# A macaron layer on one core: SwiGLU's block sums are issued one matrix later, weight sums wait behind bank copies, weight sums are cast by halves, modulation sums are spread later

## The chip, the cores and the metric

The kernel runs on one core of a Trainium2 chip. The time is the device time of one execution in microseconds (us); the number that counts is the median of the runs, and beside it stands one execution recorded by the hardware profiler. The engines in the text: PE (TensorE, matmuls), PEld (its weight loads), DVE (VectorE), ACT (ScalarE), POOL (GpSimd) and SP (SyncE, which here issues DMAs). Each engine works through its own instructions in order and waits on semaphores; SP's DMA issues wait in SP's order too.

## What is computed

One layer for 1024 positions of width 1024: a SwiGLU half step, a token mixer (two kinds of attention), and a second SwiGLU half step, each with a norm before and after and a modulation by a vector `c`. Cut to what the change touches:

```python
def swiglu(u, w_gate, w_up, w_down):          # u (1024, 1024), D_FF = 2816
    return (jax.nn.silu(u @ w_gate) * (u @ w_up)) @ w_down
...
h = x + 0.5 * g1 * postRMS(SwiGLU_1(mod1(preRMS(x))))    # FFN1
h = h + g2 * postRMS(Mixer(mod2(preRMS(h))))
h = h + 0.5 * g3 * postRMS(SwiGLU_2(mod3(preRMS(h))))    # FFN2
```

The shifts, scales and gates of `mod1` to `mod3` and g1 to g3 are rows of c @ w_ada (1024 by 9216). All arrays are float32.

## The kernel before, in words

Every float32 product runs as three matmuls on halves of the operands: `halves` makes a high part H (a cast on ACT, L217) and a low part L (a subtraction on DVE, L218), and `product` issues H·H, H·L and L·H (L293 to L295), each 128x128 by 128x512, for four blocks of 128: 12 matmuls a product.

**Matrices and pairs.** D_FF is cut into 11 pieces; for each, a pair of a gate and an up matrix is multiplied with u. `Matrix` is one of these. It does not take eight 512-products but seven, from sums of blocks of weights and of u (a scheme of Strassen's kind). `start` does the two products A11·B11 and A12·B21 (24 matmuls); then p6 (weight sum S2 with T2 of u), p5 (S1, T1), p7 (S3, T3), p3 (S4, B22) and p4 (A22, T4), 12 matmuls each: 84 matmuls a matrix, 168 a pair. T1 to T4 stay in SBUF; a matrix's S1 to S4 are made while it runs. `sums` (L315) loads the blocks (r1, r2), DVE makes `s21` = (S2, S1) at L326 and L327 and `s34` = (S3, S4) at L330 and L331, and `halves` casts both parts of `s21` in one instruction of 1024 columns, and takes its low part in another. `sums34` does the same for `s34`, `last` for A22.

**Banks.** The products accumulate in two PSUM banks in turn, `bank` and `bank2`. Each can go on only when its partial result has been read: C11 by an ACT copy (L360) and a DVE add (L368), C12 by an ACT copy (L388) and an add (L403), C22 by an ACT copy (`copy(self.c22, self.b)`, L394, which p3 waits for) and a DVE add (L398, which p4 waits for). `out` (L343) applies SiLU on ACT to a gate's block (L347) or multiplies the up block with it on DVE (L350); C21 comes straight from the bank.

**Order.** FFN1 and FFN2 run the same function. The first three pairs (six matrices, m0 to m5) all do `start` first, and `rest_first` does their other products, each matrix asking for the sums of the next one (`nxt.sums`); `done` (`follow` in `ffn`) is called between them. Pairs 3 to 10 run in a loop: `start`, then `rest`. When a pair is complete, `hidden` (L460) makes the four block sums of its SwiGLU result on DVE (L466 to L469) and stores them and three of the blocks to HBM (L472, L483); `down_sums` (L485) loads two pieces of the down weights (L488, L490), makes their four sums (L493 to L496) and stores them (L483). The down products read all that back later. `steps` is a generator of modulation sums: each step loads a row block of w_ada (`wada`, 512 KB, L86, three buffers) and reduces it with `csil` on DVE (L79, `mod_sum`); after eight steps a column of gates is stored to HBM (`g_dram`, L121). `per_pair(c)` says how many steps follow pair c.

A scheduler turns this program into one order for each engine, by dependencies, priorities and estimated costs: where the program names an operation sets its priority, not its place. `tc.issue_after(x)` keeps an operation from being placed ahead of x.

## Time and profile before

| | us |
|---|---|
| runs | 2236.72, 2235.43, 2240.99; median 2236.72 |
| profiled execution | 2242.12 (span 2240.4) |
| granted PE clock, mean | 0.989 |
| PE busy | 2155.7 (96%) |
| DVE busy | 1552.1 (69%) |
| ACT busy | 1050.0 (47%) |

FFN1 fills the span's first 700 us, the mixer the stretch up to 1570, FFN2 the rest. The gate and up products run from about 50 to 487 us and from 1575 to 2010, the down products behind them. How to read it: PE's busy share is high, so the question for each stage is when PE waited, for whom, and what that engine was doing. A row of waits reads "engine line waited for: us in total, times, longest us"; a time line row gives start and duration in us, the instruction, and in brackets the idle time before it and what ended it. A number from a busy share or from counts of matmuls is softer, since a few per cent of the matmul records are missing.

### The profile page before, as it was taken

The page shows a single profiled execution, that of the slowest core. Times are in us where ns is not written, and L with a number is a line of the kernel's source. Part 1 is how long each engine was busy: PE and PEld are TensorE (multiplying, and loading weights), DVE is VectorE, ACT ScalarE, POOL GpSimd, SP SyncE. Part 2 cuts the span into 40 slices and gives each one's busy share as a digit, 9 for nine tenths or more (in the row PEclk, how much of TensorE's full clock was granted, in tenths as well). Part 3 has the DMA queues.
Part 4 walks back from the last instruction along what each step waited for, and adds up shares of the span by engine and source line. Part 5 has one row for each costly group of instructions (what it writes and reads, how often), then busy time and mean ns, then how long its engine had stood idle before and what let it go on. Part 6 is the DMA issues. An engine that isn't in the chain of part 4 may idle for free.

```text
span 2240.4 us, 28449 instructions
## 1 busy us (share of the span) xinstructions
PE 2155.7 (96%) x10328; PEld 1780.0 (79%) x10328; DVE 1552.1 (69%) x2646; ACT 1050.0 (47%) x1893; POOL 61.5 (3%) x84
## 2 busy tenths in 40 slices
PE   6999999999998999999999999999999999999997
PEld 4777788878887877888888988788877788878886
DVE  7979767567577688576677676665985766655566
ACT  6633324235456556455455454565733333334454
POOL 0000000000000011001011000000000000000000
PEclk9999999999999999999999999999999999999999
DMA  8488635359785111110211123653474544538666
GB/s 327 146 281 280 211 130 185 127 183 328 245 291 201 50 45 46 33 54 26 70 55 64 36 94 100 236 202 128 148 239 166 184 173 144 179 111 277 215 224 213
DMA packets 139792, 361.27 MB, mean 161 GB/s; under 512 B 19458, under 2 KB 23682, under 8 KB 139651
## 3 DMA queue, kind: packets, MB, share of 16 engines
q1 hardware_dynamic: 138018, 353.68, 46.4%
q0 software_dynamic: 1632, 5.77, 0.7%
q8 instruction: 81, 1.33, 0.2%
q14 instruction: 61, 0.49, 0.1%
HBM read 270.77 MB, written 88.62 MB: 160 GB/s over the span
## 4 chain that ended last, share of the span: by engine, by line
PE 68%; DVE 19%; DMA 6%; ACT 4%; issue 3%; SPq 0%; DVEq 0%; ACTq 0%
PE bank L295 8%; PE bank L293 7%; PE bank L294 7%; PE pps L841 4%; PE pps L843 4%; PE pps L845 4%; PE bankA L581 3%; PE bankA L582 3%; PE bankA L580 3%; PE bankB L580 3%; PE bankB L582 3%; PE bankB L581 3%; DVE f L1050 2%; DVE wsL L218 2%; DMA wada<-in_wada 2%
## 5 line engine op out<-in xcount | busy, mean ns | idle before, releaser
L841 PE MATMUL pps<-uH,wsH 128*128 128x512 f32 x512 | 209.0, 408 | 0.0
L843 PE MATMUL pps<-uL,wsH 128*128 128x512 f32 x512 | 203.8, 398 | 0.0
L845 PE MATMUL pps<-uH,wsL 128*128 128x512 f32 x512 | 203.2, 397 | 0.0
L218 DVE TENSOR_TENSOR tbL<-stg,tbH 128x512 fp32r<-128x512 f32 x154 | 105.9, 689 | 97.9 <-ACT tbH L217 97.6
L217 ACT CAST tbH<-stg 128x512 fp32r<-128x512 f32 x154 | 95.6, 621 | 141.9 <-DMA stg<-d_T 98.8
L581 PE MATMUL bankA<-tbL,sbH 128*128 128x512 f32 x352 | 139.8, 397 | 6.3 <-DVE tbL L218 6.3
L580 PE MATMUL bankA<-tbH,sbH 128*128 128x512 f32 x352 | 140.1, 398 | 5.5 <-DVE y L656 5.1
L293 PE MATMUL bank<-uH,wsH 128*128 128x512 f32 x352 | 139.1, 401 | 4.1 <-ACT wsH L217 3.5
L294 PE MATMUL bank<-uL,wsH 128*128 128x512 f32 x352 | 140.2, 398 | 1.6 <-DVE uL L748 1.5
L582 PE MATMUL bankA<-tbH,sbL 128*128 128x512 f32 x352 | 139.6, 396 | 0.7 <-DVE sbL L218 0.7
L295 PE MATMUL bank<-uH,wsL 128*128 128x512 f32 x352 | 139.5, 397 | 0.6 <-DVE wsL L218 0.6
L134 DVE TENSOR_TENSOR wsL<-raw,wsH 128x1024 fp32r<-128x1024 f32 x72 | 88.0, 1222 | 68.1 <-ACT wsH L133 67.6
L217 ACT CAST wsH<-s 128x1024 fp32r<-128x1024 f32 x88 | 92.2, 1049 | 85.8 <-DVE s L327 69.8
L217 ACT CAST sbH<-stg 128x512 fp32r<-128x512 f32 (+1 forms) x176 | 98.3, 565 | 62.7 <-DMA stg<-hd_A 47.4
L218 DVE TENSOR_TENSOR sbL<-stg,sbH 128x512 fp32r<-128x512 f32 (+1 forms) x176 | 108.5, 620 | 27.0 <-ACT sbH L217 26.1
L360 ACT COPY q<-bank 128x512 f32<-128x512 f32 x44 | 25.5, 588 | 193.1 <-PE bank L295 193.1
L845 PEld LDWEIGHTS pps<-uH,wsL 128*128 128x128 f32 x512 | 96.6, 189 | 17.7
L218 DVE TENSOR_TENSOR wsL<-s,wsH 128x1024 fp32r<-128x1024 f32 x88 | 107.0, 1217 | 3.5 <-ACT wsH L217 3.2
L841 PEld LDWEIGHTS pps<-uH,wsH 128*128 128x128 f32 x512 | 97.3, 190 | 14.5
L843 PEld LDWEIGHTS pps<-uL,wsH 128*128 128x128 f32 x512 | 97.0, 189 | 14.3
L217 ACT CAST wsH<-raw 128x1024 fp32r<-128x1024 f32 (+1 forms) x88 | 73.3, 834 | 74.0 <-PE bank L294 49.8
L580 PE MATMUL bankB<-tbH,sbH 128*128 128x512 f32 x264 | 102.7, 389 | 0.0
(246 smaller groups left out, 5905.7 us busy)
## 6 DMA issues: line engine op xcount, KB each, us to landing
wada<-in_wada SPq DMA_DIRECT2D x56, 512.0 KB, 5.7
raw<-in_wg SPq DMA_DIRECT2D x50, 512.0 KB, 6.5
raw<-in_wu SPq DMA_DIRECT2D x50, 512.0 KB, 4.6
raw<-in_wd SPq DMA_DIRECT2D x44, 512.0 KB, 4.3
stg<-hd_A SPq DMA_DIRECT2D x88, 256.0 KB, 4.5
stg<-d_S SPq DMA_DIRECT2D x88, 256.0 KB, 3.5
stg<-d_T SPq DMA_DIRECT2D x88, 256.0 KB, 3.9
d_S<-s SPq DMA_DIRECT2D x40, 512.0 KB, 2.7
```

Source lines behind the costliest of these rows:

```text
L134: eng.tensor_sub(l, raw, h.bitcast(F32))
L217: ACT.copy(h, src)
L218: eng.tensor_sub(l, src, h.bitcast(F32))
L293: PE.matmul(ps, H[:, ks], bH, start=first and k == 0, stop=False, skip_group_check=not first)
L294: PE.matmul(ps, H[:, ks], bL, start=False, stop=False, skip_group_check=not first)
L295: PE.matmul(ps, L[:, ks], bH, start=False, stop=k == 3, skip_group_check=not first)
L580: PE.matmul(ps, sH[:, ts], tH, start=first, stop=False, skip_group_check=not check)
L581: PE.matmul(ps, sH[:, ts], tL, start=False, stop=False, skip_group_check=not check)
L582: PE.matmul(ps, sL[:, ts], tH, start=False, stop=last, skip_group_check=not check)
L841: PE.matmul(ps, aH, bH, start=i == 0, stop=False)
L843: PE.matmul(ps, aH, bL, start=False, stop=False)
L845: PE.matmul(ps, aL, bH, start=False, stop=i == n - 1)
```

## The change

Four edits, in gate and up products of both FFNs except the last, which concerns FFN1.

1. In `sums`, the cast of `s21` becomes two of 512 columns on ACT, S1's half first, and its low part two of 512 on DVE, S2's first: 44 more instructions on each of the two engines. `summed` is the last of the sums.
2. In `rest_first`, p7 is written ahead of `nxt.sums`, and these sums may not stand ahead of the ACT copy (`copied`) and the DVE add (`added`) of this matrix's C22.
3. `hidden` of a pair moves from behind the pair to the middle of the next pair's gate matrix (`between`, behind `m.summed`). For c = 4 the third pair's down sums go with it, as before. For the third pair `follow` no longer calls it, and the last pair's is called at the end of the loop.
4. `per_pair` of FFN1 goes from 2, then eight times 4, to 0 for the first three pairs, 5 for six pairs and 4 for one: 34 steps before and after.

```diff
@@ -325,10 +325,17 @@
             self.s34 = s34 = late.tile([P, 2, HALF], F32, name="s34", tag=tag, bufs=4)
             V.tensor_add(s21[:, 1], r2[:, 0], r2[:, 1])
             V.tensor_sub(s21[:, 0], s21[:, 1], r1[:, 0])
-            H, L = halves(wpool, s21.rearrange("p a b -> p (a b)"), "ws", 4, D)
-            self.w["S2"], self.w["S1"] = (H[:, :HALF], L[:, :HALF]), (H[:, HALF:], L[:, HALF:])
+            H = wpool.tile([P, D], F32R, name="wsH", tag="wsH", bufs=4)
+            L = wpool.tile([P, D], F32R, name="wsL", tag="wsL", bufs=4)
+            for j, n in ((1, "S1"), (0, "S2")):
+                h, l = H[:, j * HALF:(j + 1) * HALF], L[:, j * HALF:(j + 1) * HALF]
+                ACT.copy(h, s21[:, j])
+                self.w[n] = h, l
+            for j, n in ((0, "S2"), (1, "S1")):
+                h, l = self.w[n]
+                V.tensor_sub(l, s21[:, j], h.bitcast(F32))
             V.tensor_sub(s34[:, 0], r1[:, 0], r2[:, 0])
-            V.tensor_sub(s34[:, 1], r1[:, 1], s21[:, 0])
+            self.summed = V.tensor_sub(s34[:, 1], r1[:, 1], s21[:, 0])
 
         def sums34(self):
             H, L = halves(wpool, self.s34.rearrange("p a b -> p (a b)"), "ws", 4, D)
@@ -391,11 +398,11 @@
             self.b = self.psum.tile([P, HALF], F32, name="bank2", tag="pb", bufs=1)
             product(self.b, self.w["S1"], block_of("T1"), True)
             self.c22 = self.q()
-            ACT.copy(self.c22, self.b)
+            self.copied = ACT.copy(self.c22, self.b)
 
         def p7(self):
             product(self.bank, self.w["S3"], block_of("T3"), False)
-            V.tensor_add(self.c22, self.bank, self.c22)
+            self.added = V.tensor_add(self.c22, self.bank, self.c22)
             self.out("C22", self.c22)
 
         def p3(self):
@@ -446,9 +453,10 @@
             m.p6()
             done(i - 1)
             m.p5()
+            m.p7()
             if nxt is not None:
-                nxt.sums(late, True)
-            m.p7()
+                with tc.issue_after(m.copied.ins), tc.issue_after(m.added.ins):
+                    nxt.sums(late, True)
             m.p3()
             if nxt is not None:
                 nxt.sums34()
@@ -532,7 +540,7 @@
                 with tc.tile_pool(name="late", bufs=1, side="right", reuse_waits="tile") as late:
                     steps = steps_fn(late)
                     def follow(n):
-                        if n % 2:
+                        if n % 2 and n // 2 < NFIRST - 1:
                             hidden(late, n // 2, mats[n // 2][1].c, hd)
                         if n > 1:
 
@@ -547,11 +555,17 @@
                             if second:
                                 down_sums(fp, late, A[wd][c], c, hd)
                             m.start()
-                            rest(late, m, None if second or c != NFIRST + 1 else
-                                 lambda: down_sums(fp, late, A[wd][NFIRST - 1], NFIRST - 1, hd))
-                        hidden(late, c, mats[c][1].c, hd)
+
+                            def between(m=m, c=c):
+                                with tc.issue_after(m.summed.ins):
+                                    hidden(late, c - 1, mats[c - 1][1].c, hd)
+                                    if c == NFIRST + 1:
+                                        down_sums(fp, late, A[wd][NFIRST - 1], NFIRST - 1, hd)
+
+                            rest(late, m, None if second else between)
                         for _ in range(per_pair(c)):
                             next(steps, None)
+                    hidden(late, NPAIR - 1, mats[NPAIR - 1][1].c, hd)
                     for _ in steps:
                         pass
 
@@ -787,7 +801,7 @@
     def no_steps(mp):
         yield
 
-    pending = ffn("wg1", "wu1", "wd1", start0, pending0, steps1, lambda c: 2 if c == 1 else 4 if c < 10 else 0, steps1b, 0, lambda t: A["x"][t * P:(t + 1) * P, :], lambda t: h_dram[0][t])
+    pending = ffn("wg1", "wu1", "wd1", start0, pending0, steps1, lambda c: 0 if c < 3 else 5 if c < 9 else 4 if c == 9 else 0, steps1b, 0, lambda t: A["x"][t * P:(t + 1) * P, :], lambda t: h_dram[0][t])
 
     pending = mixer(locals())
```

TensorE has the same 10370 instructions in both, in the same order but for four short places: at 60 to 95 us, where the first matrices' products trade places with the transposes of T3 (these begin seven matmuls later), two places in pairs 3 and 4, where the two matmuls with T1's blocks no longer stand ahead of the matmuls with the low part of S2, and two in FFN2. In mixer and down products nothing moves. DVE's modulation sums up to the end of m5 are 18 before and 16 after.

Three places in the engines' orders. On ACT, around the C22 copy of the third pair's gate matrix (m4): `bank_1217` and `bank_1218` are the bank that p5 filled, `s_1236` and `s_1251` the next matrix's `s21`, `s_1237` and `s_1252` its `s34`. Before:

```order
L217 CAST wsH<-raw_1123 128x512
L388 COPY q<-bank 128x512
L217 CAST wsH<-s_1236 128x1024
L394 COPY q<-bank_1217 128x512
L217 CAST wsH<-s_1237 128x1024
L347 ACTIVATE q<-q 128x512
```

After:

```order
L395 COPY q<-bank 128x512
L401 COPY q<-bank_1218 128x512
L354 ACTIVATE q<-q 128x512
L332 CAST wsH<-s_1251 128x512 x2
L217 CAST wsH<-s_1252 128x1024
L354 ACTIVATE q<-bank 128x512
```

The C22 copy (L394, now L401) stood behind the cast of the next matrix's `s21` and stands ahead of its two halves (L332) now.

On DVE, at the gate matrix of pair 3: `s_1446` and `s_1421` are its `s21`, `s_1386` and `s_1441` the block sums of the third pair's SwiGLU result. Before:

```order
L466 TENSOR_TENSOR s_1386<-q 128x512
L468 TENSOR_TENSOR s_1387<-q 128x512
L467 TENSOR_TENSOR s_1386<-s_1386,q 128x512
L326 TENSOR_TENSOR s_1446<-raw_1444 128x512
L469 TENSOR_TENSOR s_1387<-q,s_1386 128x512
L327 TENSOR_TENSOR s_1446<-s_1446,raw 128x512
L330 TENSOR_TENSOR s_1447<-raw,raw_1444 128x512
L368 TENSOR_TENSOR q<-bank_1429,q 128x512
L218 TENSOR_TENSOR wsL<-s_1446,wsH 128x1024
L331 TENSOR_TENSOR s_1447<-raw,s_1446 128x512
```

After, two rows behind the gate's L327:

```order
L336 TENSOR_TENSOR wsL<-s_1421,wsH 128x512
L357 TENSOR_TENSOR q<-q 128x512
L336 TENSOR_TENSOR wsL<-s_1421,wsH 128x512
L410 TENSOR_TENSOR q<-bank_1327,q 128x512
L338 TENSOR_TENSOR s_1422<-raw,s_1421 128x512
L357 TENSOR_TENSOR q<-q 128x512
L79 ISA wada,modcol_2000<-wada,csil,colsT 128x1024
L79 ISA modcol_2000 128x1
L357 TENSOR_TENSOR q<-bank,q 128x512
L218 TENSOR_TENSOR wsL<-s_1422,wsH 128x1024
L218 TENSOR_TENSOR wsL<-raw_1419,wsH 128x512
L474 TENSOR_TENSOR s_1441<-q 128x512
```

`hidden` (L466 to L469) stood ahead of the sums and their low part; now it (from L474) begins behind the two halves of the low part (L336), two bank adds, one modulation sum and the low parts of S3, S4 and A22.

On SP, in FFN2 at pair 4's up matrix (`raw<-in_wu`): `hd_A_3` and `d_S_3` are stores of pair 3's SwiGLU result and its block sums, `d_T_2` and `d_T_4` of down sums, `raw_16265` and `raw_16327` the second load for the latter. Before:

```order
L472 DMA hd_A_3_35_16110<-q 128x512
L483 DMA d_S_3_16112<-s_16100 128x1024
L472 DMA hd_A_3_34_16108<-q 128x512
L483 DMA d_S_3_16114<-s_16101 128x1024
L488 DMA raw<-in_wd 128x1024
L490 DMA raw_16265<-in_wd 128x1024
L483 DMA d_T_2_16188<-t_16182 128x1024
L483 DMA d_T_2_16190<-t_16183 128x1024
L483 DMA d_T_4_16273<-t_16267 128x1024
L483 DMA d_T_4_16275<-t_16268 128x1024
L311 DMA raw<-in_wu 128x1024
```

After:

```order
L480 DMA hd_A_3_33_16230<-q 128x512
L496 DMA raw<-in_wd 128x1024
L480 DMA hd_A_3_35_16234<-q 128x512
L480 DMA hd_A_3_34_16232<-q 128x512
L498 DMA raw_16327<-in_wd 128x1024
L491 DMA d_S_3_16236<-s_16224 128x1024
L491 DMA d_S_3_16238<-s_16225 128x1024
L491 DMA d_T_2_16250<-t_16244 128x1024
L491 DMA d_T_2_16252<-t_16245 128x1024
L491 DMA d_T_4_16335<-t_16329 128x1024
L491 DMA d_T_4_16337<-t_16330 128x1024
L311 DMA raw<-in_wu 128x1024
```

The load of the second down weights stood behind two stores of block sums and stands ahead of them now; the up matrix's load has kept its place behind the four stores of down sums.

## The prediction

> **What bounds the kernel now.** I read the page first, then the list of what PE waits for, stage by stage, then the time line around the largest waits. From the page, the span, the busy times, four groups of instructions and a transfer:

> ```profile
> span 2240.4 us, 28449 instructions
> PE 2155.7 (96%) x10328; PEld 1780.0 (79%) x10328; DVE 1552.1 (69%) x2646; ACT 1050.0 (47%) x1893; POOL 61.5 (3%) x84
> ...
> L218 DVE TENSOR_TENSOR tbL<-stg,tbH 128x512 fp32r<-128x512 f32 x154 | 105.9, 689 | 97.9 <-ACT tbH L217 97.6
> L217 ACT CAST tbH<-stg 128x512 fp32r<-128x512 f32 x154 | 95.6, 621 | 141.9 <-DMA stg<-d_T 98.8
> ...
> L217 ACT CAST wsH<-s 128x1024 fp32r<-128x1024 f32 x88 | 92.2, 1049 | 85.8 <-DVE s L327 69.8
> ...
> L218 DVE TENSOR_TENSOR wsL<-s,wsH 128x1024 fp32r<-128x1024 f32 x88 | 107.0, 1217 | 3.5 <-ACT wsH L217 3.2
> ...
> wada<-in_wada SPq DMA_DIRECT2D x56, 512.0 KB, 5.7
> ```

> TensorE (PE) is busy 96% of the span and the change takes no matmul away, so it can only win where PE stands still. Two windows of 20 us show the price of standing still (columns: length, then busy time and count of PE, PEld, DVE, ACT, POOL, then the granted clock):

> ```profile
> 140.00:160.00 20.00, 15.99 (x69) 12.59 (x68) 17.10 (x26) 6.81 (x10) 0.00 (x0) 1.00 0.85 275
> 160.00:180.00 20.00, 17.10 (x74) 13.74 (x73) 15.06 (x25) 3.01 (x5) 0.00 (x0) 0.98 0.86 322
> 180.00:200.00 20.00, 20.00 (x85) 16.45 (x84) 18.77 (x26) 9.24 (x13) 0.00 (x0) 0.94 0.80 266
> 340.00:360.00 20.00, 20.00 (x90) 16.57 (x89) 12.95 (x18) 8.23 (x12) 0.00 (x0) 1.00 0.55 187
> 1760.00:1780.00 20.00, 18.70 (x74) 14.99 (x75) 10.70 (x14) 6.37 (x8) 0.00 (x0) 0.91 0.42 140
> ```

> A window without a wait holds 90 matmuls, 20/90 = 0.222 us each; twelve of them (a product) take 2.7 us. The others lose by idling and, in three of them, by a lowered clock besides. Next, PE's waits by stage: 92 to 170 us (first pairs), 170 to 262, 262 to 480 (later pairs), then the same of FFN2, 1610 to 1700 and 1700 to 2000 (each row: total, times, longest):

> ```profile
> PE bank L293 <- ACT q L394: 4.2, 2, 3.3
> PE bank L293 <- DVE q L398: 0.7, 1, 0.7
> ```
> ```profile
> PE bank L293 <- ACT wsH L217: 5.0, 3, 2.9
> PE bank L295 <- DVE wsL L218: 1.1, 3, 0.5
> ```
> ```profile
> PE bank L295 <- DVE wsL L218: 1.0, 6, 0.2
> ```
> ```profile
> PE tps L179 <- ACT t L252: 1.0, 1, 1.0
> PE bank L293 <- DVE q L403: 0.9, 1, 0.9
> PE bank L293 <- ACT q L388: 0.9, 1, 0.9
> PE bank L293 <- DVE q L398: 0.6, 1, 0.6
> ```
> ```profile
> PE bank L293 <- ACT wsH L217: 2.2, 1, 2.2
> PE bank L295 <- DVE wsL L218: 1.5, 8, 0.3
> ```

> **The change part by part.**

> *Sums behind the bank copies* (first pairs). The 3.3-us wait near 146 us, in time order:

> ```profile
> 142.90 1.28 DVE L79 CUSTOM_DVE_ANT_0 wada<-wada,csil,colsT 128x1024 f32<-128x1024 f32 x1 [4.03 <-DMA wada<-in_wada]
> ...
> 147.72 0.69 DVE L327 TENSOR_TENSOR s<-s,raw 128x512 f32<-128x512 f32 x1
> ```
> ```profile
> 148.49 1.04 ACT L217 CAST wsH<-s 128x1024 fp32r<-128x1024 f32 x1 [6.54 <-DVE s L327]
> 149.44 0.58 ACT L394 COPY q<-bank 128x512 f32<-128x512 f32 x1
> ```
> ```profile
> 150.08 0.50 PE L293 MATMUL bank<-B22H,wsH 128*128 128x512 f32 x1 [3.31 <-ACT q L394]
> ```

> DVE waited 4.03 us for a modulation row, so the next matrix's sum (L327) came at 147.72; ACT's queue held the cast of that sum ahead of the copy that frees the bank, and p3 waited for the copy. In the changed order the copy stands ahead of the cast. ACT is idle 6.5 us before the cast, so the copy can go the moment p5 ends. That takes away all of 4.2 us. The 0.7 beside it is the C22 add on DVE, which is now also ahead of the sums: 4.9 us in this stage.

> *SwiGLU sums a matrix later.* At the start of pair 3 the gate's S2 is late:

> ```profile
> 173.88 0.68 DVE L466 TENSOR_TENSOR s<-q 128x512 f32<-128x512 f32 x1
> ...
> 176.89 0.68 DVE L327 TENSOR_TENSOR s<-s,raw 128x512 f32<-128x512 f32 x1
> ```
> ```profile
> 178.76 0.59 PE L293 MATMUL bank<-T2H,wsH 128*128 128x512 f32 x1 [2.90 <-ACT wsH L217]
> ```

> Four 0.69-us `hidden` instructions begin before L327, 2.4 us in starts 0.60 apart. Now all four stand behind the gate's sums and casts, whose S2 comes early enough by more than the wait that is left. Of the 5.0 us (three waits of this kind: pairs 3 and 4) I take all. The halves remove the rest: p6's first block needs only S2's low part, so DVE gives it 0.69 us after the cast instead of 1.22, and ACT the cast in 0.62 instead of 1.05. The waits on `wsL` were 0.2 to 0.5 us each, less than the 0.53 gained: 1.1 + 1.0 in FFN1 and 1.5 in FFN2 go. In FFN2 the chain of the 2.2-us wait is longer:

> ```profile
> 1748.55 6.38 SPq L483 DMA_DIRECT2D d_T<-t  x4
> 1754.99 0.57 SPq L311 DMA_DIRECT2D raw<-in_wu  x1
> ```
> ```profile
> 1752.69 0.69 DVE L494 TENSOR_TENSOR t<-raw,t 128x512 f32<-128x512 f32 x1 [2.36 <-DMA raw<-in_wd]
> ```
> ```profile
> 1761.24 0.50 PE L293 MATMUL bank<-uH,wsH 128*128 128x512 f32 x1 [2.15 <-ACT wsH L217]
> ```

> SP took 6.38 us over four stores of down sums, since they wait for DVE's L494 to L496, which wait for a load; the up matrix's own load stood behind them. In the changed order the weights of these down sums are loaded behind three `hd_A` stores whose data is ready when the gate begins, and two `d_S` and four `d_T` stores still stand ahead of the up matrix's load. From the gate's start to the last of the down sums I count 9.7 us: about 2.4 for `hidden`, 5 for the load (nearest row: 5.7) and 2.4 for four adds. The up matrix needs its block 18.7 us after the gate's start (84 matmuls), so its load has 9 us where about 6 do. The 2.2 goes, and with it the clock loss of that window. Of the FFN2 row of 1610 to 1700 the ACT copy and the C22 add (0.9 + 0.6) go by the first part's reason; the T3 transposes (1.0) and one C12 add (0.9) stay.

> *Restart and clock.* A matmul after a wait shows 0.50 us instead of 0.39 to 0.40 (page mean 401 ns), 0.11 more; of the rows above some 26 waits go: 2.9 us. The clock lost (1 - 0.98) x 20 + (1 - 0.94) x 20 = 1.6 us around the 2.9-us wait and (1 - 0.91) x 20 = 1.8 around the 2.15-us one, together 3.4. The 3.31-us wait lost none (1.00). [...]

> Sum of what goes: 4.9 + 6.1 + 1.0 + 1.5 + 3.7 = 17.2 of waits, 2.9 of restarts, 3.4 of clock: 23.5 us.

> *What the halves cost.* 44 DVE and 44 ACT instructions more. Two whole casts' low parts in a row:

> ```profile
> 220.38 2.35 DVE L218 TENSOR_TENSOR wsL<-s,wsH 128x1024 fp32r<-128x1024 f32 x2
> ```

> By durations a split costs DVE 2 x 0.689 - 1.217 = 0.16 us; by starts, 0.60 apart above and 2.35 - 1.22 = 1.13 here, 0.07: 7 or 3 us over the kernel. DVE is idle 5 to 7 us of 20 in the later pairs (12.95 busy, 10.70), so PE sees none of it there. In the first pairs (17.10 and 18.77 of 20) six matrices give 0.4 to 1.0 us, counted in the next term. [...]

> *The modulation sums.* What is late next is the C22 add. The table of steps says none in the first pairs, but the order still has 16 of them there, where 18 stood, three at a time ahead of C22 adds at three places (m2, m4, and pair 3's gate). The add is needed when p4 begins, 2.7 us after p7 ends, and takes 0.69, so 2.0 us may pass; three sums of 1.28 are 3.8: up to 1.8 us lost at each, 5.4 together, if they start just as p7 ends, and none if they start 2 us earlier. They also wait for their rows: the 4.03-us wait above is such a one, so the other end is a wait of that size at a place with no slack. Two sums wait for weight loads ahead of a C22 add (pair 3's gate up to 0.7, third pair's up to 1.5), and the store of the first gate column now stands on SP ahead of two weight loads. Walking through these places with the durations above I get 0.2 + 0.8 + 1.0 + 0.7 + 1.2 + 0.5 = 4.4 us in FFN1 and 0.6 at one place in FFN2; with restarts 6.0. Ends: 0, and 12 (each place at its bound).

> *Early and unchanged.* Between 45 and 92 us the copy L388 and the transposes wait; the order there changes little (T3's transposes begin seven matmuls later):

> ```profile
> PE bank L293 <- ACT q L388: 2.0, 1, 2.0
> PE tps L179 <- ACT t L252: 1.8, 3, 1.0
> ```
> I take 0, and +-2 for the range. The 3.0-us wait at the seam to the down products,

> ```profile
> PE bankA L581 <- DVE tbL L218: 6.3, 3, 3.0
> ```

> stays: its casts still wait for the last product, whose `hidden` stands at the end as before. Mixer and down products are untouched.

> Sum: -23.5 + 6.0 = -17.5 us. The profiled execution took 2242.12, and would take 2224.6. It stands 5.4 us (0.24%) above the median of 2236.72; that gives 2219.2 for the median of the changed kernel. I state 2220.

> **The rivals.**

> *Modulation sums take the place of the waits removed.* DVE works in order, and every wait for a row now lies ahead of a C22 add rather than of a cast. For it: 4.03 us of idle at 142.90 for one row of 5.7 us median landing, three buffers only, and five sums a pair instead of four in pairs 3 to 8. Against it, DVE's waits for rows from 165 to 480 us:

> ```profile
> DVE wada L79 <- DMA wada<-in_wada: 3.9, 2, 2.0
> ```

> The longest there is no longer than the slack. Three waits of 3 to 4 us with a restart each cost 10 us: 2230.

> *Hidden anyway.* Each wait removed had another one right behind it: the S2 that comes earlier then waits for the weight load (a load took 2.36 us too long at 1752.69), the up matrix's load stays behind the same four `d_T` stores. Then only the first pairs (4.9) and the halves (3.6) gain, less 6.0 of new ones: -2.5, 2234.

> *Slower.* `hidden` and the down sums now lie in the gate matrix of each pair, on DVE between the sums and the C11 add, and five modulation sums behind them. Eight instructions of 0.60 and five of 1.28 are 11.2 us in a gate of 18.7 that also has its own adds. If from pair 3 on the C11 or C22 add comes late in each pair by the 3 us of the longest waits above, with 1.7 of clock in half of them, six pairs give 6 x 3.9 = 23 us, against 17.5 gained: 2242. It decides when such a stall returns in five pairs or more. Against it: DVE is 65% busy there (12.95 of 20).

> *Clock not tied to the waits.* If the lowered clock comes at moments of its own (for it: the 3.31-us wait kept 1.00), the 3.4 us stay, the gain is 14.1 and the time 2223: a tenth of the first case, inside its range. [...]

> **How the numbers follow.** My forecast 0.58, between 2211 and 2227; sums in place of the waits 0.22, 2226 to 2233; hidden 0.13; slower 0.07. A measurement can tell about 0.3%, 6.7 us: faster means under 2230.0, slower over 2243.4. Faster is 0.58 + 0.12 = 0.70, the same 0.10 + 0.13 = 0.23, slower 0.07. The range runs from 2209, 28 us gained (no new wait, the early stage 2 better, and 2 more where waits show only in part), to 2235, so that the first two rivals are in it.

> **What would show it.** In the changed profile: `ACT q` of the C22 copy gone from PE's waits between 92 and 170 us; no wait on `wsL` of the sums after 262 us, and none on `wsH` near 175, 218 and 240 or in the middle of FFN2; granted clock 1.00 in these windows; in their place rows on the C22 add (after L405) of 3 to 6 us in all. It is wrong if that row is over 10 us, if DVE waits on `wada` for over 20 us ahead of bank adds, or if the windows of 45 to 92 us differ by more than 3 us.

## The result, and the profile after

The changed kernel takes 2219.87 us (median; 2218.74 to 2221.86), beside 2237.16 (2235.43 to 2240.99): ratio 0.9911, 95% interval 0.9901 to 0.9922. The profiled execution took 2220.67 us, 21.45 less than the one before. From the page of the changed kernel:

```profile
span 2218.9 us, 28501 instructions
PE 2146.8 (97%) x10328; PEld 1779.1 (80%) x10328; DVE 1561.6 (70%) x2690; ACT 1058.6 (48%) x1937; POOL 61.6 (3%) x84
```

PE's matmuls are the same; DVE is busy 9.5 us longer and ACT 8.6, with 44 more instructions each. PE's waits, by the same stages as before, 92 to 170, 170 to 262 and 262 to 480 us of FFN1:

```profile
PE bank L293 <- DVE q L405: 0.9, 1, 0.9
PE bank L295 <- DVE wsL L336: 0.4, 1, 0.4
PE bank L293 <- ACT wsH L332: 0.2, 1, 0.2
```
```profile
PE bank L293 <- DVE q L405: 1.5, 2, 1.3
PE bank L293 <- ACT wsH L217: 0.6, 1, 0.6
PE bank L295 <- DVE wsL L218: 0.5, 1, 0.5
```
```profile
PE bank L293 <- ACT q L401: 2.4, 1, 2.4
```

4.9 + 6.1 + 1.0 us have become 1.5 + 2.6 + 2.4. In FFN2 the answer for 1610 to 1700 us holds no wait at all, and that for 1700 to 2000 one in the gate and up products:

```profile
PE bank L295 <- DVE wsL L218: 0.4, 1, 0.4
```

One wait is new, ahead of these, between 1570 and 1610 us:

```profile
PE bank L293 <- DVE q L375: 1.6, 1, 1.6
```

Two windows of 20 us, for the granted clock (the number after the five engines):

```profile
160.00:180.00 20.00, 20.00 (x90) 16.57 (x89) 19.04 (x31) 7.01 (x11) 0.00 (x0) 1.00 0.95 339
1760.00:1780.00 20.00, 20.00 (x90) 16.57 (x89) 16.30 (x25) 6.79 (x10) 0.00 (x0) 1.00 0.65 236
```

Where the time came from follows by setting the same matmul of the two traces side by side. FFN1's gate and up stage ends, where its down products begin, 7.95 us earlier (486.87, now 478.92); from there to the start of FFN2's products 2.05 us more are gained, nearly all of it at the seams (1.5 us is a lowered clock that lasts 3.4 us instead of 6.8 behind the same 3.0-us wait); FFN2's gate and up stage gives 10.6 (it ends at 2013.84, now 1993.25), and 0.85 lie behind it.

### The profile page after: what moved, and what is told of

It reads as the page before. It is cut to its first block, busy times and chain, and to the rows that moved or that the text cites. A ratio compares the mean times of both kernels' runs of the same rounds, so it can differ in the third digit from the quotient of the medians.

```text
span 2218.9 us, 28501 instructions
## 1 busy us (share of the span) xinstructions
PE 2146.8 (97%) x10328; PEld 1779.1 (80%) x10328; DVE 1561.6 (70%) x2690; ACT 1058.6 (48%) x1937; POOL 61.6 (3%) x84
## 4 chain that ended last, share of the span: by engine, by line
PE 76%; DVE 13%; DMA 5%; ACT 4%; issue 2%; SPq 0%; DVEq 0%; ACTq 0%
PE bank L293 10%; PE bank L294 10%; PE bank L295 10%; PE pps L855 4%; PE pps L857 4%; PE pps L859 4%; PE bankA L595 3%; PE bankA L594 3%; PE bankA L596 3%; PE bankB L594 3%; PE bankB L596 3%; PE bankB L595 3%; DVE f L1064 2%; PE vps L855 1%; PE vps L859 1%
## 5 line engine op out<-in xcount | busy, mean ns | idle before, releaser
L218 DVE TENSOR_TENSOR tbL<-stg,tbH 128x512 fp32r<-128x512 f32 x154 | 105.8, 690 | 97.3 <-ACT tbH L217 96.8
L217 ACT CAST tbH<-stg 128x512 fp32r<-128x512 f32 x154 | 95.7, 621 | 141.6 <-DMA stg<-d_T 97.2
L293 PE MATMUL bank<-uH,wsH 128*128 128x512 f32 x352 | 138.9, 401 | 4.6 <-ACT wsH L217 1.9
L295 PE MATMUL bank<-uH,wsL 128*128 128x512 f32 x352 | 139.4, 396 | 1.4 <-DVE wsL L218 1.4
L218 DVE TENSOR_TENSOR sbL<-stg,sbH 128x512 fp32r<-128x512 f32 (+1 forms) x176 | 108.6, 621 | 28.2 <-ACT sbH L217 27.2
L217 ACT CAST sbH<-stg 128x512 fp32r<-128x512 f32 (+1 forms) x176 | 98.2, 565 | 61.9 <-DMA stg<-hd_A 44.8
L217 ACT CAST wsH<-raw 128x1024 fp32r<-128x1024 f32 (+1 forms) x88 | 73.5, 836 | 103.5 <-PE bank L294 86.2
L595 PE MATMUL bankB<-tbL,sbH 128*128 128x512 f32 x264 | 102.7, 389 | 0.0
L596 PE MATMUL bankB<-tbH,sbL 128*128 128x512 f32 x264 | 102.7, 389 | 0.0
L133 ACT CAST wsH<-raw 128x1024 fp32r<-128x1024 f32 x72 | 75.5, 1049 | 52.1 <-PE pps L857 23.7
## 6 DMA issues: line engine op xcount, KB each, us to landing
wada<-in_wada SPq DMA_DIRECT2D x56, 512.0 KB, 5.6
raw<-in_wg SPq DMA_DIRECT2D x50, 512.0 KB, 7.2
raw<-in_wu SPq DMA_DIRECT2D x50, 512.0 KB, 4.8
raw<-in_wd SPq DMA_DIRECT2D x44, 512.0 KB, 5.0
d_S<-s SPq DMA_DIRECT2D x40, 512.0 KB, 5.4
```

What stands on the lines that cost most here:

```text
L217: ACT.copy(h, src)
L218: eng.tensor_sub(l, src, h.bitcast(F32))
L293: PE.matmul(ps, H[:, ks], bH, start=first and k == 0, stop=False, skip_group_check=not first)
L295: PE.matmul(ps, L[:, ks], bH, start=False, stop=k == 3, skip_group_check=not first)
L595: PE.matmul(ps, sH[:, ts], tL, start=False, stop=False, skip_group_check=not check)
L596: PE.matmul(ps, sL[:, ts], tH, start=False, stop=last, skip_group_check=not check)
```

## The experiments

All were timed against the kernel before, in three batches, in which its median was 2238.89, 2239.49 and 2241.23; so ratios are compared. Executions of one kernel spread by 3 to 12 us, so a difference of 2 us shows in the traces alone. A trace is a single execution; `old_steps` below shows by how much two of one order differ.

**One edit undone.** `whole_casts`:

```diff
-            for j, n in ((1, "S1"), (0, "S2")):
-                ...
+            H, L = halves(wpool, s21.rearrange("p a b -> p (a b)"), "ws", 4, D)
```

> The changed kernel with its first edit undone: the weight sums s21 are cast whole again (one cast of 1024, one low part of 1024), the rest stays. Theory (each edit removes its own waits, and they add up): the wait on the sums' low part comes back once a gate matrix, 0.47 us in about 5 later pairs of FFN1 and 8 of FFN2, some 6 us: 2226, and PE's list of waits shows 'PE bank L295 <- DVE wsL L218' 13 to 17 times again. Rival (the moved hidden is what made S2 early enough, and the halves only cost DVE 3 to 7 us): no such row, 2218 to 2221.

Measured: 2224.07 us, ratio 0.9925 (0.9910 to 0.9940), which is not told apart from the whole change. From 262 to 480 us one wait is left, and none on a low part:

```profile
PE bank L293 <- ACT q L394: 1.0, 1, 1.0
```

FFN1's gate and up stage ends 1.6 us earlier than with halves, FFN2's takes 1.0 us more, which is about what two executions of one order differ by. The rival was right on the waits of the later pairs: with the other edits in place they are gone without halves. In the first pairs (92 to 170 us) two waits on the low part, 1.0 us together, and one of 1.5 us on S2 stand here, where the whole change has 0.4 and 0.2.

`sums_early`:

```diff
-            m.p7()
             if nxt is not None:
-                with tc.issue_after(m.copied.ins), tc.issue_after(m.added.ins):
-                    nxt.sums(late, True)
+                nxt.sums(late, True)
+            m.p7()
             m.p3()
```

> The changed kernel with its second edit undone: in the first pairs the next matrix's sums are written ahead of p7 again and are free to stand ahead of the copies of C22. Theory: one stall of 3 to 4.5 us at about 146 us comes back (the copy of C22 behind a cast that waits for DVE, which waits for a modulation row), the rest of the profile as in the changed kernel: 2223 to 2225. Rival (the stall came from one late modulation row and its place on DVE, which other edits have moved): no stall over 1.5 us between 130 and 170 us, 2220.

Measured: 2226.80, ratio 0.9944 (0.9930 to 0.9957). A stall comes back, but on another engine and twice as long as the theory had it. PE's wait, DVE's and SP's time line in this run:

```profile
143.12 0.80 PE L293 MATMUL bank<-T4H,wsH 128*128 128x512 f32 x1 [8.09 <-DVE q L405]
```
```profile
140.03 1.29 DVE L79 CUSTOM_DVE_ANT_0 wada<-wada,csil,colsT 128x1024 f32<-128x1024 f32 x1 [7.87 <-DMA wada<-in_wada]
...
142.38 0.68 DVE L405 TENSOR_TENSOR q<-bank,q 128x512 f32<-128x512 f32 x1
```
```profile
127.42 0.38 SPq L121 DMA_DIRECT2D g_dram<-modcol  x1
127.85 1.05 SPq L86 DMA_DIRECT2D wada<-in_wada  x2
```

The modulation row that DVE waits for was issued right behind the store of a column of gates and came 12 us later. That raised a question which the last batch answers.

`hidden_at_end`:

```diff
-                            rest(late, m, None if second else between)
+                            rest(late, m, None if second or c != NFIRST + 1 else
+                                 lambda: down_sums(fp, late, A[wd][NFIRST - 1], NFIRST - 1, hd))
+                        hidden(late, c, mats[c][1].c, hd)
```

> The changed kernel with its third edit undone: the sums of the SwiGLU blocks stand behind their own pair again. Theory: the late S2 of the gates of pairs 3 and 4 (about 175, 218 and 240 us) comes back with 3 + 1.3 + 1 us less what the halves save, and the 2-us wait in FFN2 (pair 4's up matrix), while the new waits of the changed kernel in pairs 3 and 4 (1.3 on the C22 add, 0.6 + 0.5 on the up matrix's load, 2.4 on the C22 copy at 261 us) go: 2223 to 2229. Rival (the move gains in the gates what it loses at 203 to 261 us): 2218 to 2222.

Measured: 2222.84, ratio 0.9921 (0.9906 to 0.9935). PE's waits from 170 to 262 us, and the one of FFN2's up matrix:

```profile
PE bank L293 <- DVE q L405: 1.4, 1, 1.4
PE bank L293 <- ACT wsH L332: 0.7, 1, 0.7
PE bank L293 <- DVE q L375: 0.4, 1, 0.4
```
```profile
PE bank L293 <- ACT wsH L217: 3.0, 1, 3.0
```

Both theories hold in part. In FFN2 the wait is back, 4.3 us by the same matmul with its clock. In FFN1 the waits on S2 are not, 0.7 us in place of 5.0, and the stage ends 1.9 us earlier than with the whole change. All of that comes from the wait at 261 us, which is missing here; up to 248 us the stage runs 0.8 us later. The next run shows that the changed order doesn't always have that wait either, so it isn't shown that the move cost anything in FFN1.

`old_steps` puts the old table of steps back:

> The changed kernel with its fourth edit undone: the old table of modulation steps. The engines' orders are the same word for word with either table, so both theories that rest on the order expect 2220, the same waits within 0.1 us, and a difference that is only that of two executions. Rival (the table moves the modulation sums later and thereby takes the stalls near 146 us away): a stall of 3 us there comes back, 2223.

Measured: 2217.62, ratio 0.9904 (0.9889 to 0.9920), which is the whole change again. The scheduler places the modulation sums by its own priorities, and the instruction orders of all engines are the same with either table: this edit does nothing. So its trace is a second execution of the changed order, and shows how far two lie apart: up to 1.4 us either way within FFN1's stage, up to 2.5 us later on. The waits differ too. From 170 to 262 and from 262 to 480 us PE's rows on the C22 add are

```profile
PE bank L293 <- DVE q L405: 2.5, 2, 2.1
```
```profile
PE bank L293 <- DVE q L405: 0.5, 1, 0.5
```

and the 2.4-us wait on the C22 copy at 261 us is not there, though the sum in front of that copy is late here too:

```profile
260.50 0.69 DVE L326 TENSOR_TENSOR s<-raw 128x512 f32<-128x512 f32 x1 [3.78 <-DMA d_S<-s]
```

In FFN1 the C22 adds take 4.5 us in this execution (1.5 + 2.5 + 0.5) and 2.4 in the first.

**One edit alone**, on the kernel before.

> The kernel before with the first edit alone (weight sums s21 cast and lowered by halves). Theory now (the edits overlap: on DVE the halves or the moved hidden each suffice to end the 0.47-us wait of every later gate; in the first pairs only the order behind the copies keeps the C22 add from standing behind modulation rows): the 0.47-us waits go at 5 pairs of FFN1 and 8 of FFN2 (6 us); the order of the first pairs is that of the run 'sums_early', so a stall of 8 to 9 us on the C22 add stands at 138 to 147 us instead of the 3.3 on its copy; the 2.9-us wait on S2 near 176 us gets 0.5 to 1 us shorter, the 2.2-us wait in FFN2 stays: 2231 to 2237 beside 2238.9. Rival (edits add up, each with its own waits): 2232 to 2234 with the 3.3-us wait on the copy unchanged and the 2.9 unchanged.

Measured: 2232.61, ratio 0.9971 (0.9959 to 0.9983). The waits of the later gates are gone and the stall on the C22 add stands as foreseen, longer still; FFN2's wait on S2 stays (3.3 us):

```profile
PE bank L293 <- DVE q L405: 10.1, 1, 10.1
```

> The kernel before with the third edit alone (hidden a matrix later). Theory of overlapping edits: the order of the first pairs up to the third is that of the kernel before, so the 3.3-us wait on the copy near 146 us stays; the waits on S2 near 176, 218 and 240 us go, the 0.47-us waits of the later pairs go as well, without any halves, and FFN2's 2.2-us wait with its clock; new waits of 1 to 2.4 us at 200 to 265 us: 2224 to 2229. Rival (the halves end the waits of the later pairs): the rows 'PE bank L295 <- DVE wsL L218' stay 13 to 17 times, 2230 to 2233.

Measured: 2224.29, ratio 0.9927 (0.9912 to 0.9942): the larger part of the whole gain. FFN1's gate and up stage ends as early as with all four edits (478.9 us in both). From 262 to 480 us there is no wait, without halves; the first pairs and FFN1's S2:

```profile
PE bank L293 <- ACT q L394: 3.9, 2, 2.9
```
```profile
PE bank L293 <- DVE q L398: 0.9, 2, 0.6
PE bank L293 <- ACT wsH L217: 0.9, 1, 0.9
```

> The kernel before with the second edit alone (the next matrix's sums behind the C22 copy and add). Theory: the 3.3-us wait near 146 us goes; the modulation sums are drawn ahead of the third pair's last C22 add, so that DVE's queue at the gate of pair 3 is two or three modulation sums shorter and the 2.9-us wait on S2 near 176 us falls to under 1 us with no hidden moved; the 0.47-us waits of 13 later gates and FFN2's 2.2 us stay: 2228 to 2232. Rival (hidden ahead of the gate's sums is the cause of the wait near 176 us): it stays at 2 to 3 us with its clock loss, 2233 to 2236.

Measured: 2233.03, ratio 0.9970 (0.9958 to 0.9982). The copy's wait near 146 us is gone, but a wait of 1.6 us on S2 near 139 us is new, and the waits from 92 to 170 us fall only from 4.9 to 3.4. S2's waits from 170 to 262 us have fallen from 5.0 to 2.2 us, though `hidden` still stands ahead; the small waits stay:

```profile
PE bank L293 <- ACT wsH L217: 2.2, 2, 1.2
PE bank L295 <- DVE wsL L218: 1.5, 4, 0.5
```
```profile
PE bank L295 <- DVE wsL L218: 0.9, 5, 0.2
```

So S2 was late behind `hidden` and the modulation sums together in DVE's order: with the sums ahead of the last C22 add 2.2 us are left, with `hidden` moved 0.9 (`only_hidden`), and with `hidden` in its old place but the other edits done 0.7 (`hidden_at_end`). Alone the three edits gain 0.29, 0.73 and 0.30%, 1.32 in sum; together 0.89: they overlap. In FFN2 the wait on S2 in the middle of the stage (2.0 to 3.3 us) is gone in every kernel here with the third edit in FFN2 and stays in every one without it.

**Modulation sums held back.**

```diff
+                        with tc.issue_after(first[-1].added.ins):
                             for _ in range(per_pair(c)):
                                 next(steps, None)
```

> The changed kernel with its modulation sums really held back: none of them may stand ahead of the last C22 add of the first six matrices; they follow in pairs 3 to 6. Theory (the waits left over in the first pairs, 0.9 + 0.4 + 0.2 us, come from modulation sums and their rows ahead of the C22 adds): those go, the waits at 200 to 262 us (C22 adds, the up matrix's load, the C22 copy) stay or grow by up to 2 us, since all 32 sums now fall there: 2217 to 2221. Rival (held sums pile up in pairs 3 to 6 and delay C22 and C11 adds by 3 us in three or four places): 2226 to 2232.

Measured: 2221.16, ratio 0.9912 (0.9899 to 0.9925): no different. From 92 to 170 us PE has no wait left, and from 170 to 262 the sums now stand ahead of a C22 and a C11 add:

```profile
PE bank L293 <- DVE q L405: 3.9, 2, 3.6
PE bank L293 <- DVE q L375: 1.4, 1, 1.4
```

At the end of FFN1's stage 0.6 us are gained: 3.1 won by 167 us, 4.9 given back by 248 us, and 2.5 from the wait at 261 us, which is missing here as in `old_steps`.

**The store of 4-byte packets.** The last four kernels store the column of gates as 128 rows of 32 bytes, and DVE reads it back in that order where the norm is multiplied (L206):

```diff
-        SP.dma_start(row.rearrange("o (k p) -> p (o k)", p=P), g)
+        SP.dma_start(row.rearrange("o (p k) -> p (o k)", p=P), g)
...
-            V.scalar_tensor_tensor(y[:, c], y[:, c], r, g[:, c], ALU.mult, ALU.mult)
+            yc = y[:, c].rearrange("q (k p) -> q k p", p=P)
+            gc = g.rearrange("q (p k) -> q k p", p=P)[:, c.start // P:c.stop // P]
+            V.scalar_tensor_tensor(yc, yc, r, gc, ALU.mult, ALU.mult)
```

With this edit every engine has its instructions in the same order as in the kernel without it, in all three kernels where only this differs (`before_packed`, `early_packed`, `packed`).

> The kernel before with one edit of my own and none of the change: the column of gates is stored as 128 rows of 32 bytes instead of 1024 single numbers of 4 bytes, and the DVE multiplication that uses it reads it in that order. Theory (the store of 1024 4-byte packets, 8 to 11 us to landing, holds up the loads behind it on SP's queue, and that delay is what DVE's 4.03-us wait at 142.90 us and PE's 3.3-us wait at 146 us come from): the store lands in under 4 us, the waits of DVE for a modulation row near 140 us and of PE near 146 us go or fall under 1 us, 2233 to 2236 beside 2239. Rival (the loads are late by their number, eight of 512 KB in 20 us, and the store only stands beside them): 2238 to 2240, waits unchanged.

Measured: 2250.93, ratio 1.0052 (1.0037 to 1.0066). The theory on the stall is right, and the time is wrong for another reason, below. Transfers between 130 and 144 us (count, KB each, median us to landing), of the kernel before and then of this one, and this one's whole list of PE's waits from 92 to 170 us:

```profile
wada<-in_wada SPq DMA_DIRECT2D x3, 512.0 KB, 10.8
```
```profile
wada<-in_wada SPq DMA_DIRECT2D x4, 512.0 KB, 5.2
```
```profile
PE bank L295 <- DVE q L400: 0.2, 1, 0.2
```

With the loads in the same place and no other edit, the 4.9 us of waits are 0.2. S2's waits from 170 to 262 us stay (4.9 us), and so does FFN2's (2.0): those are not the store's.

> The run 'sums_early' (the change without the sums behind the C22 copy and add) with the same packed store. Theory: its 8.1-us wait on the C22 add at 135 to 143 us, which began with a modulation row issued 0.4 us behind the store, falls under 2 us; 2226.8 becomes 2216 to 2220, that is, the second edit is no longer needed. Rival: the wait stays over 5 us, 2225 to 2228.

Measured: 2233.95, ratio 0.9973 (0.9964 to 0.9981). The 8.1-us wait on the C22 add is gone, and FFN1's stage ends 2.7 us earlier than in the changed kernel, without the second edit:

```profile
PE bank L295 <- DVE q L407: 1.3, 2, 1.0
```

> The changed kernel with the packed store. Theory: the 0.9-us wait on the C22 add near 134 us goes, and so does the 2.4-us wait at 261 us, since the load and the stores issued at 245 to 256 us behind the second such store land in 5 us instead of 9: 3 us less, 2215 to 2218. Rival (the 2.4 us come from the number of stores and from four buffers for block sums): 2218 to 2221 with the wait at 261 us.

Measured: 2229.79, ratio 0.9952 (0.9938 to 0.9965). FFN1's stage ends 6.45 us earlier than in the changed kernel: 3.8 us by 248 us, and 2.7 more since the wait at 261 us is gone. That wait, in the changed kernel, with DVE's, ACT's and the transfers issued from 244 to 262 us:

```profile
261.94 0.69 DVE L326 TENSOR_TENSOR s<-raw 128x512 f32<-128x512 f32 x1 [6.30 <-DMA d_S<-s]
```
```profile
262.75 0.62 ACT L332 CAST wsH<-s 128x512 fp32r<-128x512 f32 x1 [6.06 <-DVE s L326]
263.27 0.58 ACT L401 COPY q<-bank 128x512 f32<-128x512 f32 x1
```
```profile
d_S<-s SPq DMA_DIRECT2D x2, 512.0 KB, 8.7
...
g_dram<-modcol SPq DMA_DIRECT2D x1, 4.0 KB, 11.0
```

The four tiles for block sums (tag `s`) serve `hidden`, the down sums and the weight sums; the next weight sum waits until a store of `hidden` has landed, and ACT's queue holds the C22 copy behind the cast of that sum. With the packed store the same transfers took:

```profile
d_S<-s SPq DMA_DIRECT2D x2, 512.0 KB, 5.3
...
g_dram<-modcol SPq DMA_DIRECT2D x1, 4.0 KB, 1.4
```

That the store makes these transfers late is borne out by the other runs: two `d_S` stores took 8.7, 9.1 and 9.3 us behind it (`old_steps` and `whole_casts` are the other two), and 4.6 to 5.6 where it was packed or stood elsewhere (`early_packed`, `steps_held`, `only_hidden`). How much of the delay reaches PE is another matter: 2.4 us in the changed kernel, 1.0 in `whole_casts`, nothing in `old_steps`.

What the packed store costs stands in the multiplication, changed kernel and packed one, and in PE's wait at the first seam (4.0 in the changed kernel):

```profile
L206 DVE SCALAR_TENSOR_TENSOR y<-y,rs,grow 128x1024 f32<-128x1024 f32 x22 | 28.2, 1283 | 0.5
```
```profile
L208 DVE SCALAR_TENSOR_TENSOR y<-y,rs,grow 128x1024 f32<-128x1024 f32 x22 | 48.4, 2202 | 0.5
...
PE bankA L596 <- DVE y L672: 9.6, 1, 9.6
```

Reading every eighth number makes one of these 2202 ns instead of 1283. DVE works 20 us longer on it, and from the end of FFN1's gate and up stage to the last matmul 14.0 us are lost. The wait shown accounts for 5.6 of them; that the rest too is this multiplication, with little beside it to cover it at the seams, is likely but not shown.

> The changed kernel with the packed store, and hidden behind its own pair in FFN1 as before the change, a matrix later in FFN2 alone. Theory (moving hidden bought nothing in FFN1 once the other two edits stand, and cost the waits at 226 and 261 us; in FFN2 it bought 4.3 us): 2214 to 2217, as fast as 'packed' or 1 to 2 us faster. Rival (the waits on S2 at 176 and 218 us come back): 2219 to 2224.

Measured: 2232.83, ratio 0.9968 (0.9957 to 0.9979): the theory's time fails by the cost just told. FFN1's stage ends 0.4 us later than in `packed`; 1.7 us come back at the gate of pair 4 and are made up elsewhere. With the store out of the way, the place of `hidden` in FFN1 makes no difference that these traces can tell.

## Why the prediction was right, and where its steps were not

**The sum.** 17.5 us were forecast, and the medians are 17.3 apart. The profiled pair, from whose rows the terms come, is 21.45 apart, so that the agreement to 0.2 us is in part luck. In this pair the waits of the rows named fell by 19.1 - 6.9 = 12.2 us, or 10.6 with the new 1.6-us wait in FFN2; forecast were 17.2 gone and some 5 new, 12.2. The clock gave more than the 3.4 counted: both lowered stretches counted (at 179 and 1763 us) went, and of those outside these stages two got 3.4 us shorter and one longer, 10.2 us of half clock less in all, worth 5.1. What lies outside was not earned by the change: see the last section.

**By stage it was off, and three terms were missed.** FFN2 gave 10.6 us where its terms (1.5 + 3.7 of waits, their restarts, 1.8 of clock, less 0.6) came to about 7.6; FFN1 8.0, where its terms came to about 10.

The first term is the restart. It was counted by the length of a matmul, 0.11 us more behind a wait. But matmuls overlap: one starts every 0.227 us and lasts 0.39, and a row of waits counts only from the end of one to the start of the next. So each wait also costs the 0.16 us of overlap. At each later gate the wait of 0.17 us (0.2 in its row) cost 0.45 by the starts in the two traces; for the 26 waits that went, 4.2 us were not counted, less 1.6 for some ten new ones.

The second is the new waits of FFN1, sized at 4.4 and measured 6.5 and, in the second execution (`old_steps`), 6.1. "What is late next is the C22 add" was half right: the C22 adds took 2.4 us in the one, less than the 3 to 6 us that were named as the sign, and 4.5 in the other. The third was not looked for: in the first execution 2.4 us is an ACT copy behind a cast that waits for a store to land. Of a step that is moved I had counted the instructions and DMAs, not the buffers that it holds.

**Sums behind the bank copies** did remove the wait at 146 us, by the chain told (`only_first`: 4.6 us by the matmuls around it, with 1.6 us lost to a new wait just ahead). But the chain was followed back only to a late modulation row. Its cause was a store of 4 KB one instruction ahead on SP; pack that alone and the wait goes with no change of the order (`before_packed`).

**SwiGLU sums a matrix later.** FFN2's 2.2-us wait and its clock are this edit's alone (`hidden_at_end`: 4.3 us back; `only_halves` and `only_first` keep the wait), by SP's order as worked out. In FFN1 the S2 waits were put down to `hidden`; the first two edits together remove most of them too (5.0 to 0.7), and once they stand, no gain of the move is left to see there.

**The halves.** "The halves remove the rest" is wrong as a cause. `only_hidden` has no wait on the low part after 262 us and no halves; `whole_casts` neither. They suffice alone in the later pairs, and add nothing measurable to the rest in time; only in the first pairs are the waits smaller with them (1.5 us, 3.2 in `whole_casts`). Their price on DVE, 4.5 us of busy time by `only_halves` against the kernel before and 6.0 by `whole_casts` against the changed one, is 0.10 to 0.14 a matrix, inside the 0.07 to 0.16 taken, and lies beside PE's work: `only_halves` has no wait of PE from 262 to 480 us.

**Modulation sums.** 18 and 16 in the first pairs were read as the fourth edit working weakly. The difference is the other edits'; the fourth moves nothing, which no rival allowed for.

**The rivals.** New stalls of 3 to 4 us behind modulation rows were real, but in kernels with only part of the change (8.1 and 10.1 us). The change has none since its second edit keeps the C22 add ahead of the sums. The slower case, C11 or C22 adds late in each pair, did not occur: between 262 and 480 us there is one wait in all. "Hidden anyway" did not hold in FFN2, where 0.4 us of waits are left behind 1610 us, and the two lowered stretches went with their waits, against "Clock not tied to the waits".

## What to carry to other kernels

Follow a late transfer back to what stands ahead of it in its queue, and look at packet sizes there: the second edit reordered engines around a delay that one store of 4-byte packets made (10.8 us for the loads behind it, 5.2 with packets of 32 bytes). When a step is moved, list the buffers that it holds beside its instructions, and the stores that must land before they are free. Take edits one at a time and one away: these three overlap so far that one alone gave most of the gain, and a fourth did nothing. Before a wait in one trace is laid to an edit, look at a second execution of the same order: the largest new wait here was in one of two. A version that would join both, the packed store with one copy that puts the row in order instead of 26 strided reads, wasn't tried.

## What the runs showed of the hardware

**A store of 1024 packets of 4 bytes took 8.4 and 11.0 us to land** in the changed kernel (two of the three; the trace doesn't show the first one's landing), 9.1 and 9.5 in the kernel before; as 128 packets of 32 bytes the second took 1.4 (`packed`). Between 130 and 144 us 1120 packets under 512 bytes moved in the kernel before and 276 in `before_packed`, and the 512-KB loads issued behind the store took 10.8 and 5.2 us: the transfers behind it suffered too.
